# S5 scan of a hybrid encoder: two groups per pass of the array, chunk innermost in the state, one step for both directions

## Chip, cores and metric

The kernel runs on one core of a Trainium2 chip. The metric is the device time of one execution in microseconds. Three runs of the kernel before took 2780.14, 2782.51 and 2787.14 us; the median is 2782.51 us.

## What is computed

The reference is one layer of an encoder over 2304 tokens (256 of a prompt, 2048 of a sample). Its input projection feeds two mixers. One is a gated recurrence (HGRN heads). The other, which the change touches, is a complex diagonal state-space layer (S5) with 32 groups of 16 channels, 64 complex states in each group and two directions. Then come an output projection and an MLP.

```python
bu_re = jnp.einsum('bsgc,gpc->bsgp', u, bb_re)      # and bu_im
_, _, xr, xi = lax.associative_scan(combine, (a_re, a_im, bu_re, bu_im), axis=1)
return jnp.einsum('bsgp,gcp->bsgc', xr, c_re) - jnp.einsum('bsgp,gcp->bsgc', xi, c_im)
...
y_b = _flip(s5_direction(_flip(ug), ...))           # the other direction
```

## The kernel before

Time is cut into 288 chunks of 8 tokens (`NJ`), of which the first 32 (`JP`) are the prompt. The S5 layer then has three parts.

**Chunk inputs** (`s5_in`, lines 552 to 565). For each of 32 groups `g` the sync queue (SP) loads the chunked inputs `ug` (line 559) and, for every second group, the weights `wt` of a pair (line 555). For the real and the imaginary part one matmul (line 562) gives a PSUM tile of 128 partitions by 288 chunks: 64 states of the forward direction over 64 of the backward one. ScalarE copies the upper half into the forward state tile (line 564), VectorE the lower half into the backward one (line 565). A state tile is `[128 partitions, 289 slots, re/im, 16 group pairs]`; a partition is (parity of the group, state). The 288 elements that one copy writes therefore lie 32 words apart, and the 32 elements that belong to one slot lie side by side.

**Scan** (`s5_step`, lines 569 to 580, called in lines 588 to 594). A step takes a direction from one slot to the next with three VectorE operations: `pr = prev * decay`, `cur += pr[0]`, `swp += pr[1]` with real and imaginary parts swapped. The second addition works on the elements that the first has just written, and the next step's product reads them again. While the prompt lasts (k = 1 to 30) an operation carries prompt and sample together: 128 elements in the product, 64 in each addition. For the 224 steps after that (k = 31 to 254) it carries the sample alone: 64 and 32. Both directions step in turn, each in its own tile, so there are six operations per k, and three chained ones always have those of the other direction to be mixed with.

**Outputs** (lines 637 to 657). For every group ScalarE copies the forward states of all slots (line 649) and VectorE the backward ones (line 650) into `xg`, in which the slots lie side by side; three matmuls (lines 652 to 654) add to one PSUM tile, ScalarE copies it out (`yg`, line 656), and the GpSimd queue stores it.

Beside the scan TensorE does the projections of `stage2_v` and `stage2_gq` (lines 599 to 628): 15 tiles of v, then 32 tiles of output gates and queries, whose results ScalarE copies out of three PSUM banks tagged `fl`. The query weights `wqq` (line 625) are split into two parts by ScalarE (`whi`, line 161) and VectorE (`wlo`, line 162). Gate and query tiles of the last two blocks (`late`, line 717) may run once their `h` is loaded, as far as the three `fl` banks go.

The order of the instructions on an engine is not the program's: a planner simulates the program with its own costs (`schedule_with_timeline_sim=True`, line 1340) and puts each instruction where it is ready in that simulation. Each engine then works strictly in that order.

Of the kernel before, what the change touches and what calls it, by code (L numbers as in the profile page):

```python
# [9 lines left out]
F32 = mybir.dt.float32  # L10
# [19 lines left out]
G = 32  # L30
# [14 lines left out]
def hybrid_trunk_kernel(  # L45
# [17 lines left out]
    def order(ins, after, kind=mybir.DependencyClass.NoSync):  # L63
        """Places an instruction behind another one."""
        tc.add_manual_dep(ins.ins, after.ins.name, mybir.DependencyInfo(kind, mybir.DependencyReason.DATA), reason="order of issue")
# [16 lines left out]
    def act(o, i, f, **kw):  # L82
        S.activation(out=o, in_=i, func=f, **kw)  # L83

# [126 lines left out]
    # =====================================================================  # L211
    # stage 1: norm1, h^T, u projection; tables of the S5 layer; chunk inputs
    # =====================================================================
# [62 lines left out]
    def s5_tables():  # L276
# [109 lines left out]
        # decay over one chunk, arranged for the scans: partitions (group parity, state), [kind, re/im, group pair]  # L386
        adec = []
        for d in range(2):
            ad = const.tile([P, 2, 2, G // 2], F32, name=f"adec{d}")
            for q in range(2):  # L390
                o, i = ad[q * 64:(q + 1) * 64], ap[d * 64:(d + 1) * 64, :, LC, q::2]
                for ri in range(2):
                    V.tensor_copy(out=o[:, 0, ri], in_=i[:, 0])
                V.tensor_copy(out=o[:, 1, 0], in_=i[:, 1])
                ts(o[:, 1, 1], i[:, 1], -1.0, op0=ALU.mult)
            adec.append(ad)

        # input matrix of the discretised system
# [16 lines left out]
        # powers arranged by position in the chunk, per direction  # L415
# [14 lines left out]
        # B of the discretised system, and C, with all groups  # L430
# [10 lines left out]
        def quad(o):  # L441
# [9 lines left out]
            # chunk input weights  # L451
# [11 lines left out]
            # output weights  # L463
# [12 lines left out]
            # kernel of every lag: sum over states of B' (C a^n)  # L476
# [29 lines left out]
    # v: blocks from V1 on beside the norms, the others under the scan; NL blocks of queries and output gates  # L506
    # under the S5 outputs; S5 half of the output projection of NE blocks before the backward heads
# [30 lines left out]
    # ---- S5 chunk inputs and states; partitions (group parity, state), [slot, re/im, group pair].  # L538
    # forward: chunk j enters at slot j + 1; backward: at slot j. A chunk's incoming state lies one slot before / after.
# [7 lines left out]
    stt_ = [sp.tile([P, NJ + 1, 2, GH], F32, name=f"st5_{d}") for d in range(2)]  # L547
# [4 lines left out]
    def s5_in(g):  # L552
        if g % 2 == 0:
            wt = tmp2.tile([P, 4, P], F32, name="wt", tag="wt")
            nc.sync.dma_start(out=wt, in_=win_d[g // 2])
            hx["wt"] = wt
        wt = hx["wt"]
        ug = tmp2.tile([P, NJ], F32, name="ug", tag="ug", bufs=4)
        nc.sync.dma_start(out=ug, in_=u_d[g // 8][:, (g % 8) * C16:(g % 8 + 1) * C16, :])
        for ri in range(2):  # L560
            pi = ptile("mm" if (2 * g + ri) % 5 < 3 else "sx", NJ)
            hx["mark", g] = T.matmul(pi, wt[:, 2 * (g % 2) + ri], ug, start=True, stop=True)
            qs = slice((g % 2) * 64, (g % 2 + 1) * 64)
            act(stt_[0][qs, 1:NJ + 1, ri, g // 2], pi[:64], AF.Copy)
            V.tensor_copy(out=stt_[1][qs, 0:NJ, ri, g // 2], in_=pi[64:])

    SL = 2 * GH

    def s5_step(d, src, dst, nq):
        """One chunk of the scan: sample, and beside it prompt (nq = 2) while that lasts."""  # L570
        gap = (JP if d == 0 else NJ - JP) * SL
        s0, d0 = (src * SL, dst * SL)
        prev = view(stt_[d], s0, [[gap, nq], [0, 2], [1, SL]])
        cur = view(stt_[d], d0, [[gap, nq], [1, SL]])
        swp = view(stt_[d], d0, [[gap, nq], [GH, 2], [1, GH]])
        pr = tmp2.tile([P, 2, 2, SL], F32, name="pr", tag=f"pr{d}")[:, :nq]
        ad = view(adec[d], 0, [[0, nq], [SL, 2], [1, SL]])
        tt(pr, prev, ad, ALU.mult)
        tt(cur, cur, pr[:, :, 0], ALU.add)
        tt(swp, swp, view(pr, SL + GH, [[2 * SL, nq], [-GH, 2], [1, GH]]), ALU.add)  # L580

    for g in range(G):
        s5_in(g)
    for j in (0, JP):
        V.memset(stt_[0][:, j], 0.0)
    for j in (JP, NJ):
        V.memset(stt_[1][:, j], 0.0)
    for k in range(1, NJ - JP - 1):
        if k < JP - 1:
            s5_step(0, k, k + 1, 2)  # L590
            s5_step(1, JP - k, JP - k - 1, 2)
        else:
            s5_step(0, JP + k, JP + k + 1, 1)
            s5_step(1, NJ - k, NJ - k - 1, 1)

    # =====================================================================
    # stage 2: v and the output gate of the HGRN heads
    # =====================================================================
# [31 lines left out]
    # =====================================================================  # L630
    # stage 3: S5 outputs
    # =====================================================================
# [4 lines left out]
    for g in range(G):  # L637
# [11 lines left out]
        act(xg[:64], stt_[0][qs, 0:NJ, :, g // 2].rearrange("p j r -> p r j"), AF.Copy)  # L649
        V.tensor_copy(out=xg[64:], in_=stt_[1][qs, 1:NJ + 1, :, g // 2].rearrange("p j r -> p r j"))  # L650
# [70 lines left out]
    for b in range(NB):  # L721
# [33 lines left out]
        # mean square of every token; its root scales this half of the output projection  # L755
# [14 lines left out]
    # =====================================================================  # L770
    # stage 4: HGRN heads, two at a time
    # =====================================================================
# [8 lines left out]
    # lower bounds of the gates: softmax over the layers  # L781
# [20 lines left out]
    def chain(pair, b, h, q, pf, pb):  # L802
        """Gates, and operands of every level: decayed queries and keys."""
# [16 lines left out]
        for m in (1, 2, 4, 8, 16, 32, 64):  # L820
            nb = TB // m
            j = nb // 2
            # rows as the level wants them: by the parity of the block of m tokens
# [26 lines left out]
    def mix(pair, b, h, sel, KQ, ptot):  # L850
        """Attention of the chunks in [source, target] layout, chunk states, forward outputs."""
# [28 lines left out]
        # keys decayed to the chunk's edges -> [token, key], then the states the chunks add  # L880
# [39 lines left out]
    def backward(pair, b):  # L920
        """States from the right, full outputs, norm of every head."""
# [32 lines left out]
    def gate_out(pair, b, outs, r):  # L954
        """Scale by the norm, transpose, gate."""
# [12 lines left out]
    # software pipeline: the projections of the next (block, head) run under the chain of this one  # L968
# [20 lines left out]
    # the output projection of the S5 half and the residual; the heads' half follows  # L989
# [74 lines left out]
    # =====================================================================  # L1064
    # stage 5: output projection of the heads' half, norm2
    # =====================================================================
# [4 lines left out]
    # The products of the MLP by the Winograd form of Strassen's algorithm, one level: seven block products for eight.  # L1071
    # C = A B in blocks: P1 = A11 B11, P2 = A12 B21, P3 = S4 B22, P4 = A22 T4, P5 = S1 T1, P6 = S2 T2, P7 = S3 T3 with
    # S1 = A21 + A22, S2 = S1 - A11, S3 = A11 - A21, S4 = A12 - S2; T1 = B12 - B11, T2 = B22 - T1, T3 = B22 - B12,
    # T4 = B21 - T2; U2 = P1 + P6, U3 = U2 + P7; C11 = P1 + P2, C12 = U2 + P5 + P3, C21 = U3 + P4, C22 = U3 + P5.
    # A is [token, feature], cut by blocks of tokens and halves of the features; B the weights.
# [3 lines left out]
    def s_terms(a, eng=V):  # L1079
        """a: [A21, A11, A12, A22, ...] -> S1 .. S4 behind them."""  # L1080
# [14 lines left out]
    def prep(third, j):  # L1095
        """norm2, transposed: the A operands of the first product, to DRAM."""
# [68 lines left out]
    # =====================================================================  # L1165
    # stage 6: MLP, first product
    # =====================================================================
# [64 lines left out]
    # =====================================================================  # L1232
    # MLP, second product, and the final norm
    # =====================================================================
# [109 lines left out]
```

## Time and profile before

| | |
|---|---|
| median of three runs | 2782.51 us |
| the profiled execution, from first to last instruction | 2785.5 us |
| TensorE matmul busy | 2627.3 us (94%) |
| VectorE busy | 2088.9 us (75%) |
| ScalarE busy | 1411.8 us (51%) |
| chunk inputs, about | 222 to 289 us of the span |
| scan, about | 289 to 516 us |
| S5 outputs, about | 516 to 579 us |

The profiled execution is 3.0 us (0.11%) above the median. Busy times count every instruction from start to end, and neighbours on one engine overlap by a part of their length, so the distance of two starts is shorter than an instruction where nothing is waited for. L12 is line 12 of the kernel, but most VectorE and ScalarE instructions stand under the lines of the helpers `tt` (L68) and `act` (L83); the names of the tiles tell them apart: `pr` and `st` are the scan.

### The profile page before, as it was taken

The page shows a single profiled execution, that of the slowest core. Times are in us where ns is not written, and L with a number is a line of the kernel's source. Part 1 is how long each engine was busy: PE and PEld are TensorE (multiplying, and loading weights), DVE is VectorE, ACT ScalarE, POOL GpSimd, SP SyncE. Part 2 cuts the span into 40 slices and gives each one's busy share as a digit, 9 for nine tenths or more (in the row PEclk, how much of TensorE's full clock was granted, in tenths as well). Part 3 has the DMA queues.
Part 4 walks back from the last instruction along what each step waited for, and adds up shares of the span by engine and source line. Part 5 has one row for each costly group of instructions (what it writes and reads, how often), then busy time and mean ns, then how long its engine had stood idle before and what let it go on. Part 6 is the DMA issues. An engine that isn't in the chain of part 4 may idle for free.

```text
span 2785.5 us, 48587 instructions
## 1 busy us (share of the span) xinstructions
PE 2627.3 (94%) x17590; PEld 2346.9 (84%) x17590; DVE 2088.9 (75%) x5451; ACT 1411.8 (51%) x2632; POOL 665.8 (24%) x853
## 2 busy tenths in 40 slices
PE   6897999889999998999999899989999999999998
PEld 6774899679999887788989899989998888888887
DVE  6666879657899797566999999999986455555564
ACT  5535121476788685345775554564554333344342
POOL 1231233332111112222354344344441000000000
PEclk9999999999999999999999999999999999999999
DMA  9757653687556456799686776687649555765562
GB/s 265 250 189 228 220 179 140 193 252 212 177 182 206 155 192 224 260 327 350 233 281 241 248 276 222 208 283 247 224 149 344 173 170 170 255 229 196 192 218 82
DMA packets 345304, 615.63 MB, mean 221 GB/s; under 512 B 66376, under 2 KB 229576, under 8 KB 345064
## 3 DMA queue, kind: packets, MB, share of 16 engines
q1 hardware_dynamic: 275608, 328.55, 37.6%
q0 software_dynamic: 69456, 283.98, 28.2%
q8 instruction: 139, 2.28, 0.3%
q14 instruction: 101, 0.83, 0.1%
HBM read 409.80 MB, written 202.60 MB: 220 GB/s over the span
## 4 chain that ended last, share of the span: by engine, by line
PE 44%; issue 21%; DVE 19%; ACT 6%; DMA 6%; POOL 4%; SPq 1%; POOLq 0%; ACTq 0%; DVEq 0%
DVE w L68 5%; PE pm L174 5%; PE pm L177 5%; PE pm L178 5%; DVE w1t L68 5%; PE px_g L178 3%; PE px_g L174 3%; PE px_g L177 3%; PE px_fl L174 2%; PE px_fl L178 2%; PE px_fl L177 2%; PE px_tr L174 2%; PE px_tr L178 2%; PE px_tr L177 2%; DVE c L68 2%
## 5 line engine op out<-in xcount | busy, mean ns | idle before, releaser
L68 DVE TENSOR_TENSOR sl<-gt,sh 128x1280 fp32r<-128x1280 f32 (+1 forms) x112 | 153.7, 1373 | 290.7 <-ACT sh L83 289.6
L83 ACT ACTIVATE sh<-gt 128x1280 fp32r<-128x1280 f32 (+1 forms) x112 | 130.7, 1167 | 392.9 <-PE pm L177 150.3
L174 PE MATMUL px_f<-oh,w 128*128 128x384 f32 x672 | 228.0, 340 | 19.8 <-DVE u L68 16.1
L174 PE MATMUL pm<-oh,w 128*128 128x384 f32 x672 | 227.4, 339 | 3.6 <-DVE u L68 2.8
L178 PE MATMUL pm<-oh,w 128*128 128x384 f32 x672 | 227.1, 338 | 2.5 <-DVE w L68 2.4
L177 PE MATMUL px_f<-ol,w 128*128 128x384 f32 x672 | 226.9, 338 | 2.7 <-DVE ol L68 2.7
L177 PE MATMUL pm<-ol,w 128*128 128x384 f32 x672 | 227.6, 339 | 1.7 <-DVE ol L68 1.7
L178 PE MATMUL px_f<-oh,w 128*128 128x384 f32 x672 | 226.5, 337 | 0.9 <-DVE w L68 0.9
L174 PE MATMUL pm<-hh,whi 128*128 128x384 f32 x576 | 200.5, 351 | 9.3 <-ACT sg L83 3.9
L177 PE MATMUL pm<-hl,whi 128*128 128x384 f32 x576 | 200.9, 349 | 0.0
L178 PE MATMUL pm<-hh,wlo 128*128 128x384 f32 x576 | 197.9, 346 | 0.0
L83 ACT ACTIVATE sel<-KQ 128x384 f32<-128x384 f32 (+1 forms) x312 | 168.6, 560 | 52.0 <-DVE KQ L68 50.2
L83 ACT ACTIVATE w<-w1t 128x512 fp32r<-128x512 f32 x192 | 115.4, 620 | 131.7 <-DVE w1t L68 130.0
L83 ACT ACTIVATE c<-c 128x384 f32<-128x384 f32 x192 | 98.2, 516 | 140.2 <-DVE c L68 139.9
L68 DVE TENSOR_TENSOR KQ<-KQ,Fl 128x384 f32<-128x384 f32 x288 | 154.4, 552 | 10.8 <-ACT sel L83 8.7
L1268 POOL DMA_DIRECT2D out_dram<-x x14 | 7.5, 533 | 601.2 <-DVE rs_y L68 484.2
L68 DVE TENSOR_TENSOR w<-w1t,w 128x512 fp32r<-128x512 f32 x192 | 137.2, 716 | 18.4 <-ACT w L83 18.4
L68 DVE TENSOR_TENSOR st<-st,pr 128x32 f32<-128x32 f32 (+1 forms) x1016 | 149.7, 203 | 0.0
L174 PE MATMUL pm<-th,sh 128*128 128x512 f32 x384 | 149.7, 391 | 0.0
L177 PE MATMUL pm<-tl,sh 128*128 128x512 f32 x384 | 149.4, 389 | 0.0
L178 PE MATMUL pm<-th,sl 128*128 128x512 f32 x384 | 149.4, 389 | 0.0
L174 PEld LDWEIGHTS px_f<-oh,w 128*128 128x128 f32 x672 | 126.4, 188 | 24.9 <-issue 19.9
(365 smaller groups left out, 7973.8 us busy)
## 6 DMA issues: line engine op xcount, KB each, us to landing
w1r<-in_w_ff_dram SPq DMA_DIRECT2D x48, 1024.0 KB
gt<-s_d SPq DMA_DIRECT2D x112, 384.0 KB
xg<-in_w_ff_dram SPq DMA_DIRECT2D x80, 512.0 KB
s_d<-his POOLq DMA_DIRECT2D x48, 768.0 KB, 5.0
hh<-h_hi POOLq DMA_DIRECT2D x46, 768.0 KB, 7.5
hl<-h_lo POOLq DMA_DIRECT2D x46, 768.0 KB, 6.7
xg<-t_d SPq DMA_DIRECT2D x64, 512.0 KB
s_d<-hid POOLq DMA_DIRECT2D x48, 576.0 KB, 7.1
```

The costliest lines, as they stand in the source:

```text
L68: ins = V.tensor_tensor(out=o, in0=a, in1=b, op=op)
L83: S.activation(out=o, in_=i, func=f, **kw)
L174: ins = T.matmul(o, ah, bh, start=first, stop=False)
L177: T.matmul(o, ah, bl, start=False, stop=False)
L178: return T.matmul(o, al, bh, start=False, stop=last)
L1268: queue.dma_start(out=rows(yp, ys, t), in_=xt)
```

## The change

The state is one tile `[128, direction, re/im and group pair (32), 289 slots]`, with the slots innermost. `s5_in` takes a pair of groups at once: for each of re/im and direction, two matmuls of 64 weight columns each write the two halves of one PSUM tile, at columns 0 and 64 of the array; the whole tile then goes to the state in one copy, of 128 partitions and 288 elements side by side, by ScalarE for the forward and by VectorE for the backward direction. A step of the scan reads and writes elements that lie 289 words apart. For k = 1 to 30 there is still one step for each direction; for k = 31 to 254 one step of three operations takes both, 128 elements in the product and 64 in each addition. The decay is one tile for both directions. The copies into `xg` read slots that lie side by side. Comments are taken out, so that line numbers stay close.

```diff
-    stt_ = [sp.tile([P, NJ + 1, 2, GH], F32, name=f"st5_{d}") for d in range(2)]
+    SL, NS = 2 * GH, NJ + 1
+    stt_ = sp.tile([P, 2, SL, NS], F32, name="st5")
...
-    def s5_in(g):
...
-        for ri in range(2):
-            pi = ptile("mm" if (2 * g + ri) % 5 < 3 else "sx", NJ)
-            hx["mark", g] = T.matmul(pi, wt[:, 2 * (g % 2) + ri], ug, start=True, stop=True)
-            qs = slice((g % 2) * 64, (g % 2 + 1) * 64)
-            act(stt_[0][qs, 1:NJ + 1, ri, g // 2], pi[:64], AF.Copy)
-            V.tensor_copy(out=stt_[1][qs, 0:NJ, ri, g // 2], in_=pi[64:])
+    def s5_in(g2):
+        wt = tmp2.tile([P, 4, P], F32, name="wt", tag="wt")
+        nc.sync.dma_start(out=wt, in_=win_d[g2])
+        ug = []
+        for g in (2 * g2, 2 * g2 + 1):
+            ug.append(tmp2.tile([P, NJ], F32, name="ug", tag="ug", bufs=4))
+            nc.sync.dma_start(out=ug[-1], in_=u_d[g // 8][:, (g % 8) * C16:(g % 8 + 1) * C16, :])
+        for ri in range(2):
+            for d in range(2):
+                pi = ptile("mm" if (4 * g2 + 2 * ri + d) % 5 < 3 else "sx", NJ)
+                for q in range(2):
+                    hx["mark", 2 * g2 + q] = T.matmul(pi[q * 64:(q + 1) * 64], wt[:, 2 * q + ri, d * 64:(d + 1) * 64], ug[q], start=True, stop=True, tile_position=(0, q * 64))
+                o = stt_[:, d, ri * GH + g2, 1 - d:NJ + 1 - d]
+                if d:
+                    V.tensor_copy(out=o, in_=pi)
+                else:
+                    act(o, pi, AF.Copy)
...
+    def s5_step(src, dst, gap, gap2, ad):
+        prev = view(stt_, src, [[gap, 2], [0, 2], [NS, SL]])
+        cur = view(stt_, dst, [[gap2, 2], [NS, SL]])
+        swp = view(stt_, dst, [[gap2, 2], [GH * NS, 2], [NS, GH]])
+        pr = tmp2.tile([P, 2, 2, SL], F32, name="pr", tag="pr")
         tt(pr, prev, ad, ALU.mult)
         tt(cur, cur, pr[:, :, 0], ALU.add)
-        tt(swp, swp, view(pr, SL + GH, [[2 * SL, nq], [-GH, 2], [1, GH]]), ALU.add)
+        tt(swp, swp, view(pr, SL + GH, [[2 * SL, 2], [-GH, 2], [1, GH]]), ALU.add)
...
         else:
-            s5_step(0, JP + k, JP + k + 1, 1)
-            s5_step(1, NJ - k, NJ - k - 1, 1)
+            f, b = JP + k, DS + NJ - k
+            s5_step(f, f + 1, b - f, b - f - 2, view(adec, 0, [[2 * SL, 2], [SL, 2], [1, SL]]))
...
-        act(xg[:64], stt_[0][qs, 0:NJ, :, g // 2].rearrange("p j r -> p r j"), AF.Copy)
-        V.tensor_copy(out=xg[64:], in_=stt_[1][qs, 1:NJ + 1, :, g // 2].rearrange("p j r -> p r j"))
+        act(xg[:64], stt_[qs, 0, g // 2::GH, 0:NJ], AF.Copy)
+        V.tensor_copy(out=xg[64:], in_=stt_[qs, 1, g // 2::GH, 1:NJ + 1])
```

## Rows read from the trace of the kernel before

**Rows 1.** Busy time of each engine in three stretches: inputs, projections under the scan, outputs.
```profile
core 0: us, PE busy (x) PEld busy (x) DVE busy (x) ACT busy (x) POOL busy (x), PEclk, DMA share, GB/s
222.00:289.00 67.00, 49.50 (x183) 33.24 (x183) 37.67 (x71) 37.77 (x65) 5.39 (x10) 0.97 0.72 226
289.00:499.00 210.00, 206.03 (x1077) 192.18 (x1076) 191.88 (x1384) 37.19 (x67) 60.15 (x95) 0.99 0.50 174
...
517.00:579.00 62.00, 49.51 (x180) 33.80 (x180) 20.54 (x32) 48.20 (x62) 25.12 (x38) 0.96 0.78 234
```
**Rows 2.** Timeline of ScalarE and TensorE, end of scan: start, length, engine, line, tiles [idle before].
```profile
494.50 0.49 ACT L83 ACTIVATE gt<-px_fl 128x384 f32<-128x384 f32 x1 [3.69 <-PE px_fl L178]
498.66 0.49 ACT L83 ACTIVATE gt<-px_fl 128x384 f32<-128x384 f32 x1 [3.67 <-PE px_fl L178]
516.39 1.24 ACT L83 ACTIVATE xg<-st 64x576 f32<-64x576 f32 x1 [17.24 <-DVE st L68]
...
511.88 0.72 PE L652 MATMUL pm<-ug,tm 128*128 128x288 f32 x2
517.68 0.85 PE L653 MATMUL pm<-xg,wc 128*128 128x288 f32 x1 [5.08 <-ACT xg L83]
```
**Rows 3.** Timeline of VectorE, six operations per step: k under 31, then k over 30.
```profile
289.55 0.48 DVE L68 TENSOR_TENSOR pr<-st,adec 128x128 f32<-128x128 f32 x2
289.95 0.62 DVE L68 TENSOR_TENSOR st<-st,pr 128x64 f32<-128x64 f32 x4
290.50 0.48 DVE L68 TENSOR_TENSOR pr<-st,adec 128x128 f32<-128x128 f32 x2
...
359.95 0.36 DVE L68 TENSOR_TENSOR pr<-st,adec 128x64 f32<-128x64 f32 x2
360.22 0.54 DVE L68 TENSOR_TENSOR st<-st,pr 128x32 f32<-128x32 f32 x4
360.68 0.35 DVE L68 TENSOR_TENSOR pr<-st,adec 128x64 f32<-128x64 f32 x2
```
**Rows 4.** Who waited for whom, 289 to 517 us: total, times, longest.
```profile
DVE wlo L68 <- ACT whi L83: 18.1, 2, 9.4
```
**Rows 5.** Groups of 222 to 289 us by shape: count, busy us, mean ns, idle before.
```profile
L83 ACT ACTIVATE st<-pm 64x288 f32<-64x288 f32 x39 | 23.6, 665 | 20.0 <-PE pm L562 19.8
L565 DVE COPY st<-pm 64x288 f32<-64x288 f32 x39 | 23.4, 649 | 17.3 <-ACT st L83 17.0
L562 PE MATMUL pm<-ug,wt 128*128 128x288 f32 x76 | 22.8, 418 | 7.1 <-DMA wt<-win_d 4.6 <-DVE st L565 2.5
```
**Rows 6.** Groups of 516 to 578 us by shape, ScalarE.
```profile
L83 ACT ACTIVATE xg<-st 64x576 f32<-64x576 f32 x32 | 38.5, 1203 | 18.0 <-DVE st L68 17.2
...
L83 ACT ACTIVATE yg<-pm 128x288 f32<-128x288 f32 x29 | 11.6, 399 | 13.0 <-PE pm L654 12.9
```
**Rows 7.** Timeline of the inputs: a load of weights and the matmuls that wait for it.
```profile
248.29 0.32 SPq L555 DMA_DIRECT2D wt<-win_d  x1
...
252.23 1.70 PE L562 MATMUL pm<-ug,wt 128*128 128x288 f32 x6 [1.34 <-DMA wt<-win_d]
```
**Rows 8.** Timeline of TensorE in the heads: matmuls on quarters of the array's columns.
```profile
721.78 1.03 PE L861 MATMUL px_lv<-sel 128*32 128x32 f32 x96
```
**Rows 9.** Timeline of VectorE: a chained pair at the end, and two unrelated neighbours early.
```profile
2778.28 0.15 DVE L198 CAST rs_t<-rs_x 128x1 f32<-128x1 int32 x1
2778.47 0.15 DVE L77 TENSOR_SCALAR rs_y<-rs_t 128x1 int32<-128x1 f32 x1
...
43.12 0.19 DVE L68 TENSOR_TENSOR t<-t,t 128x32 f32<-128x32 f32 x1
43.23 0.18 DVE L288 COPY lim<-px_tr 128x32 f32<-128x32 f32 x1
```
**Rows 10.** The tile `z`: shortest, median and longest ns of an operation, first and last start.
```profile
L68 DVE TENSOR_TENSOR z<-yt,ga x24: 822/862/1585, 589.9 to 676.0; 128x384 f32<-128x384 f32 x24
...
L68 DVE TENSOR_TENSOR z<-z,gate x24: 541/552/560, 611.7 to 704.7; 128x384 f32<-128x384 f32 x24
```
**Rows 11.** Groups of VectorE over the whole span by shape: every second word, in place.
```profile
L68 DVE TENSOR_TENSOR KQ<-KQ,F 128x192 f32<-128x192 f32 x48 | 15.0, 352 | 0.0
```

More of the change, by code (lines that the diff above doesn't have):

```diff
@@ L384, in s5_tables @@
                  b_re, b_im, ap[:, 0, 1:1 + n, :], ap[:, 1, 1:1 + n, :], pw1[:, :n], pw2[:, :n])
-        adec = []
+        adec = const.tile([P, 2, 2, 2, G // 2], F32, name="adec")
         for d in range(2):
-            ad = const.tile([P, 2, 2, G // 2], F32, name=f"adec{d}")
+            ad = adec[:, d]
             for q in range(2):
@@ L395, in s5_tables @@
                 ts(o[:, 1, 1], i[:, 1], -1.0, op0=ALU.mult)
-            adec.append(ad)
         den, nr, cr, ci = pt("den"), pt("nr"), pt("cr"), pt("ci")
@@ L550, in hybrid_trunk_kernel @@
     wg = [col_unit(w_in, 2048 + h * P) for h in range(NH)]
-    def s5_in(g):
[L553 to L559, printed above, removed]
-        for ri in range(2):
-            pi = ptile("mm" if (2 * g + ri) % 5 < 3 else "sx", NJ)
-            hx["mark", g] = T.matmul(pi, wt[:, 2 * (g % 2) + ri], ug, start=True, stop=True)
-            qs = slice((g % 2) * 64, (g % 2 + 1) * 64)
-            act(stt_[0][qs, 1:NJ + 1, ri, g // 2], pi[:64], AF.Copy)
-            V.tensor_copy(out=stt_[1][qs, 0:NJ, ri, g // 2], in_=pi[64:])
@@ L567, in hybrid_trunk_kernel @@
[L567 to L577, printed above, removed]
+    def s5_in(g2):
[5 more added lines that the diff above has]
+            nc.sync.dma_start(out=ug[-1], in_=u_d[g // 8][:, (g % 8) * C16:(g % 8 + 1) * C16, :])
+        for ri in range(2):
+            for d in range(2):
[7 more added lines that the diff above has]
+                    act(o, pi, AF.Copy)
@@ L578, in s5_step @@
+    def s5_step(src, dst, gap, gap2, ad):
[3 more added lines that the diff above has]
+        pr = tmp2.tile([P, 2, 2, SL], F32, name="pr", tag="pr")
         tt(pr, prev, ad, ALU.mult)
         tt(cur, cur, pr[:, :, 0], ALU.add)
-        tt(swp, swp, view(pr, SL + GH, [[2 * SL, nq], [-GH, 2], [1, GH]]), ALU.add)
-    for g in range(G):
-        s5_in(g)
+        tt(swp, swp, view(pr, SL + GH, [[2 * SL, 2], [-GH, 2], [1, GH]]), ALU.add)
@@ L584, in hybrid_trunk_kernel @@
+    for g2 in range(GH):
+        s5_in(g2)
     for j in (0, JP):
-        V.memset(stt_[0][:, j], 0.0)
+        V.memset(stt_[:, 0, :, j], 0.0)
     for j in (JP, NJ):
-        V.memset(stt_[1][:, j], 0.0)
+        V.memset(stt_[:, 1, :, j], 0.0)
+    DS = SL * NS
     for k in range(1, NJ - JP - 1):
         if k < JP - 1:
-            s5_step(0, k, k + 1, 2)
-            s5_step(1, JP - k, JP - k - 1, 2)
-        else:
-            s5_step(0, JP + k, JP + k + 1, 1)
-            s5_step(1, NJ - k, NJ - k - 1, 1)
+            for d in range(2):
+                at, gap = (k, JP) if d == 0 else (DS + JP - k, NJ - JP)
+                s5_step(at, at + 1 - 2 * d, gap, gap, view(adec, d * 2 * SL, [[0, 2], [SL, 2], [1, SL]]))
+        else:
+            f, b = JP + k, DS + NJ - k
+            s5_step(f, f + 1, b - f, b - f - 2, view(adec, 0, [[2 * SL, 2], [SL, 2], [1, SL]]))
```

## Prediction

> **What bounds the kernel now.** I read the busy times by stretch first. From 289 to 499 us, beside the scan, both TensorE (206 of 210 us) and VectorE (192) are full [rows 1]. Which of them sets the end is seen in the timeline at 516 us: TensorE has finished its projections at 511.9, starts the first product that needs no state, and then stands for 5.1 us until `xg` comes; ScalarE's `xg` has waited 17.2 us for the scan's last addition [rows 2]. So the scan ends last, but by little: a shorter scan gains some 6 us before TensorE's own work is the bound, and a longer one costs every microsecond. From 517 to 579 us neither TensorE (49.5 of 62 us) nor ScalarE (48.2) is full; after that TensorE is, so a shift of 579 us goes through to the end.
>
> The scan itself: a step of six operations takes 0.95 us while k is under 31 (from `pr` at 289.55 to `pr` at 290.50) and 0.73 us after (359.95 to 360.68) [rows 3]. 30 and 224 of them make 28.5 + 163 = 191 us of the 228 between 288.6 and 516.4. Of the rest, 18.1 us are two waits of VectorE at `wlo`, for ScalarE's half of the query weights [rows 4].
>
> **Chunk inputs.** Now a copy writes words 32 apart and takes 665 ns on ScalarE and 649 ns on VectorE, 64 each, and VectorE's waits for ScalarE's of the same PSUM tile [rows 5]. After, each engine makes 32 copies into neighbouring words; ScalarE's `yg`, of that shape, takes 399 ns [rows 6]. That takes some 30 us off each engine. But the copies are not all that paces this part. A weight load issued at 248.29 (when its buffer came free) had its matmuls waiting until 252.23 [rows 7]; there are two buffers, so a pair of groups needs about half of these 3.9 us and half of the matmuls' own 2 us, near 3 at best, against 67 / 16 = 4.2 us on the average, in a stretch in which the DMA engines are busy for 0.72 of the time [rows 1]; I take the loads for the larger part of it. The matmuls become twice as many with half the columns. In the heads 96 passes on 32 columns of the array take 1.03 us, 10.7 ns each [rows 8], where a pass over 32 moving columns at the rate of `pm<-ug,wt` (1.70 us for six of 288 [rows 7]) would take 31 ns; so neighbours on other columns do run together, and I take the pair at the price of the one it replaces. I put the part at **-4 us**, between -19 (every pair at 3 us) and +15 (pairs run one after the other: 31 us more on TensorE, half of it in its gaps).
>
> **The scan, k over 30.** Three operations of 128, 64 and 64 elements take the place of six of 64 and 32. This halves the instructions, but each now needs the one right before it. What that costs: in the last norm one-element operations of 0.15 us, each on the result of the one before, start 0.19 us apart, 40 ns more than their length; unrelated 0.19 us neighbours start 0.11 us apart [rows 9]. In the kernel before, an operation of the other direction stands in between and the 0.73 us are the second kind. From 128x384 in 552 ns [rows 10] and 128x192 in 352 ns [rows 11] an addition or product costs 152 ns and 1.04 ns per element: 285 ns for 128 elements, 219 ns for 64. Chained: 325 + 259 + 259 = 0.84 us, already above 0.73.
>
> Then the stride. `z<-yt,ga` reads both sources 48 words apart and takes 822 to 862 ns, `z<-z,gate` of the same shape on neighbouring words 552 [rows 10]: 0.70 to 0.81 ns per element more. The DVE copy that writes 32 words apart fits: 649 ns against 152 + 300 [rows 5]. No row has a read and a write 289 words apart. Below, it costs nothing: `KQ<-KQ,F` in place on every second word takes the 352 ns that the other rows lead to [rows 11]. Above, the penalties of read and write add to 1.5 ns per element. I take 0.75 for the product (reads apart, writes together) and 0.81 for the additions, as `z` is nearest in stride and number of streams: 0.42 + 0.31 + 0.31 = 1.04 us. Over 224 steps that is 234 us instead of 163: **+71 us**, between +26 (no penalty) and +92 (1.14 us).
>
> The Trainium skill's page "Vector Engine (DVE) Microarchitecture Reference", section "Measured stream behaviour on trn2", has a harsher figure for some strides: 2.5 ns per column in place of 1.05 where a stream steps 24 words. By that a step would be an estimated 1.2 us and the scan another 36 us longer; it also lists 1.7 to 2.0 for wider hops, near my rows.
>
> **The scan, k under 31.** Still six operations in two independent chains, so only the stride is added: 0.10 us for each of two products, 0.05 for each of four additions, 0.40 us times 30: **+12 us** (0 to +18).
>
> **VectorE's queue.** `wlo` and the waits on it stay in the queue. The first 9.4 us come because VectorE is there early; a slower VectorE comes later: **-9 us** (-18 to 0). The query projections then get their weights late, but TensorE has over 60 us to spare by then. Query loads on SP and stores on POOL keep their order and only gain time.
>
> **Outputs.** `xg` on ScalarE takes 1203 ns now [rows 6]; on neighbouring words 576 elements should take about 690 (399 plus 288 at 1 ns), 16 us less in all. But TensorE needs six passes of up to 0.28 us [rows 7] per group, as much as ScalarE's two copies take now, and a group takes 62 / 32 = 1.94 us, more than either: **-3 us** (-10 to 0). What was hidden by the scan stays hidden; TensorE now stands idle from about 512 to the scan's end.
>
> **Sum.** -4 + 71 + 12 - 9 - 3 = +67 us on the profiled 2785.5, so 2852.5; less the 3.0 us by which the profile stands over the median, 2849.5 us. The scan would end near 580 us in place of 516.
>
> **Rivals.**
> *Half the operations, half the scan (faster).* If chained operations start as close as unrelated ones and the stride is free, a step costs 0.20 + 2 x 0.14 = 0.48 us, by the starts at 289.55 to 290.50 [rows 3]. The scan is 56 us shorter; the gain stops at the 6 us of TensorE's wait, the 4 of the inputs and some 8 of the outputs' gaps that projections can fill: about 2766 us. It decides if the 40 ns behind the chained pair are not paid. The Trainium skill says so on "VectorE: DVE Perf Modes", section "The DRAIN you can't avoid": with or without semaphores a chain took the same time, and "the semaphore costs nothing extra here". The trace disagrees: 0.19 against 0.11 us [rows 9]. 10%.
>
> *Only one of the two costs is paid (about no change).* Chained but without a stride penalty: +26 - 9 - 4 - 3, 2793 us; with the penalty but not chained (0.30 + 2 x 0.19 = 0.68 us a step): -11 + 12 - 9 - 7, about 2770 us. For it speaks that 352 ns on every second word; against it, `z`. 10%.
>
> *The planned order turns against it (slower still).* Its own simulation orders the instructions. Before, it put the last projections ahead of `xg` on ScalarE, as things then went [rows 2]. If it believes in a scan shorter by the 0.48 us steps (135 us for 191), it puts `xg` into ScalarE's queue at about 445 us. ScalarE then stands there until the scan really ends; three `fl` banks fill, and some ten projections of 4.17 us (494.50 to 498.66 [rows 2]) are left for afterwards: 42 us, of which the outputs' 12.5 us of TensorE gaps [rows 1] take a part. 29 us on top: about 2878 us. 20%.
>
> *The halves do not run side by side.* Then the change doesn't do what its words say: +15 in place of -4, about 2868 us. Against it, 10.7 ns a pass [rows 8]. 5%.
>
> **Numbers.** The forecast has 55%: 2849.5 us. The range takes in the planned order, the bounds of the stride and the upper half of the second rival, not the faster case: 2790 to 2892 us. About 0.3% (8 us) is what a measurement of this kernel can tell from no change. Faster by more: the 10% of the first rival and a little of the second, 0.11. Within: 0.08. Slower: 0.81.
>
> **What would show it.** In the profile after: `pr` and `st` of 128x128 and 128x64 with starts 0.42 and 0.31 us apart and no other operation between; lengths of about 0.38 and 0.27 us; TensorE idle before the first `xg` for tens of microseconds; evictions of 128x288 near 0.4 us; `xg` on ScalarE near 0.7 us. It is wrong if the long steps take 0.7 us or less, if TensorE never waits for the scan, or if ScalarE's last `gt` stand behind `xg`.

## The result, and the profile after

The changed kernel takes **2861.62 us** (median of four runs, 2858.61 to 2869.1) against 2782.17 for the kernel before on the same chip: a ratio of **1.0289**, 95% interval 1.0271 to 1.0308. The change costs 79 us; 2849.5 was predicted, 12 us less. The profiled execution lasts 2861.7 us from first to last instruction, 76.2 more than the one of before.

The busy times by stretch, columns as in [rows 1]: inputs, projections under the scan, the rest of the scan, outputs.

```profile
222.00:289.00 67.00, 55.55 (x271) 31.84 (x270) 13.65 (x32) 12.13 (x30) 3.82 (x8) 0.97 0.63 194
289.00:499.00 210.00, 204.63 (x1049) 188.15 (x1048) 191.83 (x609) 37.28 (x67) 58.44 (x91) 0.98 0.52 178
517.00:585.00 68.00, 4.49 (x26) 4.03 (x24) 61.19 (x199) 0.00 (x0) 0.00 (x0) 0.57 0.02 3
585.00:700.00 115.00, 97.16 (x423) 79.45 (x424) 49.70 (x87) 68.50 (x133) 42.73 (x63) 0.93 0.81 236
```

The third row is new: from 521.5 us until the scan's end VectorE is alone at work, hardly a transfer runs (3 GB/s), and TensorE's granted clock averages 0.57, most of the stretch at the lower of its two levels (1.2 GHz in place of 2.4). The timeline of ScalarE and TensorE at the scan's end shows who waits (answers to [rows 2]):

```profile
508.61 0.49 ACT L83 ACTIVATE gt<-px_fl 128x384 f32<-128x384 f32 x1 [3.67 <-PE px_fl L178]
585.89 2.10 ACT L83 ACTIVATE xg<-st 64x576 f32<-64x576 f32 x3 [76.79 <-DVE st L68]
...
586.63 1.33 PE L656 MATMUL pm<-xg,wc 128*128 128x288 f32 x2 [65.14 <-ACT xg L83]
...
595.05 0.65 PE L655 MATMUL pm<-ug,tm 128*128 128x288 f32 x2
```

The first `xg` comes at 585.9 instead of 516.4, and TensorE stands for 65 us where it stood for 5. The last `gt` lies ahead of `xg`, so nothing that could run under the scan is stuck behind it. VectorE's timeline gives the steps, k under 31 and k over 30 (answers to [rows 3]):

```profile
294.74 0.70 DVE L68 TENSOR_TENSOR pr<-st,adec 128x128 f32<-128x128 f32 x2
295.33 0.83 DVE L68 TENSOR_TENSOR st<-st,pr 128x64 f32<-128x64 f32 x4
296.06 0.70 DVE L68 TENSOR_TENSOR pr<-st,adec 128x128 f32<-128x128 f32 x2
...
439.80 0.40 DVE L68 TENSOR_TENSOR pr<-st,adec 128x128 f32<-128x128 f32 x1
440.23 0.59 DVE L68 TENSOR_TENSOR st<-st,pr 128x64 f32<-128x64 f32 x2
440.86 0.39 DVE L68 TENSOR_TENSOR pr<-st,adec 128x128 f32<-128x128 f32 x1
```

The short step (k under 31) takes 1.32 us (before 0.95), the long one (k over 30) 1.06 us (before 0.73), and in the long one each operation starts only after the one before has ended. Who waited for whom: VectorE from 289 to 590 us (answers to [rows 4]), then TensorE from 222 to 660 us:

```profile
DVE wlo L68 <- ACT whi L83: 0.2, 1, 0.2
...
PE pm L656 <- ACT xg L83: 65.9, 2, 65.1
PE pm L656 <- DMA wc<-wc_d: 10.8, 7, 2.3
```

Groups by shape: evictions and matmuls of the inputs, and ScalarE's copies of the outputs (answers to [rows 5, 6]):

```profile
L83 ACT ACTIVATE st<-pm 128x288 f32<-128x288 f32 x19 | 7.7, 412 | 46.5 <-PE pm L564 37.3 <-PE px_sx L564 4.4 <-DMA win_d<-wt 4.4
L567 DVE COPY st<-pm 128x288 f32<-128x288 f32 x19 | 8.7, 457 | 37.9 <-PE pm L564 37.9
L564 PE MATMUL pm<-ug,wt 128*64 128x288 f32 x145 | 35.0, 412 | 8.2 <-DMA wt<-win_d 4.9 <-DMA ug<-u_d 3.1 <-ACT st L83 0.2
L83 ACT ACTIVATE xg<-st 64x576 f32<-64x576 f32 x32 | 21.8, 683 | 77.5 <-DVE st L68 76.8
```

The copies did get cheap: 0.41 and 0.46 us, half as many, and `xg` 683 ns instead of 1203. But both engines now wait for TensorE in the inputs, and nothing of it reaches the end.

**Where the 76.2 us lie.** The scan begins at 293.43 instead of 288.62 (+4.8). It lasts 292.4 us instead of 227.8 (+64.7): the 30 short steps make +11.6, the waits at `wlo` -17.9, and what is left, +71.0, is the 224 long steps. From the scan's end to the next projection the outputs take 72.3 us instead of 69.1 (+3.2). The last +3.5 come later. All this is read from one profile of each kernel; how far the small parts vary between profiles is said below where they matter.

### The profile page after: what moved, and what is told of

The parts are those of the page before. It is cut to its first block, busy times and chain, and to the rows that moved or that the text cites. A ratio compares the mean times of both kernels' runs of the same rounds, so it can differ in the third digit from the quotient of the medians.

```text
span 2861.7 us, 48080 instructions
## 1 busy us (share of the span) xinstructions
PE 2648.1 (93%) x17718; PEld 2356.1 (82%) x17718; DVE 2119.5 (74%) x4747; ACT 1371.0 (48%) x2600; POOL 664.5 (23%) x853
## 5 line engine op out<-in xcount | busy, mean ns | idle before, releaser
L68 DVE TENSOR_TENSOR st<-st,pr 128x64 f32<-128x64 f32 x568 | 157.8, 296 | 15.3
L1085 POOL TENSOR_TENSOR his<-hid 128x384 f32<-128x384 f32 x96 | 136.6, 1442 | 47.1 <-ACT hid L83 33.1
```

Of the source, the lines that this page charges most:

```text
L68: ins = V.tensor_tensor(out=o, in0=a, in1=b, op=op)
L1085: eng.tensor_tensor(out=a[o], in0=a[x], in1=a[y], op=op)
```

## Experiments

The theory: a long step is longer for two reasons, each paid: three operations that wait for one another, and words 289 apart. The rivals: only the chain, or only the distance. The first three kernels undo one or both in the changed kernel and leave its inputs as they are.

**Words side by side, the chain kept** (`chain_near`).

```diff
-    stt_ = sp.tile([P, 2, SL, NS], F32, name="st5")
+    stt_ = sp.tile([P, 2, NS, SL], F32, name="st5")
...
-        cur = view(stt_, dst, [[gap2, 2], [NS, SL]])
+        cur = view(stt_, dst * SL, [[gap2 * SL, 2], [1, SL]])
```

> The changed kernel with the state turned back so that the 32 elements of a slot lie side by side (copies into the state and out of it step 32 words again); one step of three chained operations for both directions stays. Theory (chain and far words both cost): a step of k over 30 takes 0.84 us in place of 1.04, one of k under 31 0.95 in place of 1.32, the scan is 56 us shorter, the time about 2810 us. Rival 'far words alone' (chaining is free): the step falls to 0.48 us, the scan is over 100 us shorter, TensorE is the bound, about 2775 us. Rival 'chain alone': the step stays at 1.04 us and the time near 2861 us.

**Words far apart, each direction by itself for every k** (`apart_far`): six operations, with a `pr` for each direction.

```diff
+    for k in range(1, NJ - JP - 1):
+        for d in range(2):
...
+                at, gap, nq = (JP + k, JP, 1) if d == 0 else (DS + NJ - k, JP, 1)
+            s5_step(at, at + 1 - 2 * d, gap, nq, view(adec, d * 2 * SL, [[0, nq], [SL, 2], [1, SL]]), d)
```

> The changed kernel with the chunk innermost as it is, but each direction stepping by itself for all k, so that six operations in two independent chains alternate. Theory: no operation waits for its neighbour; a step of k over 30 takes 0.90 us (0.73 and 0.5 to 0.75 ns for each of 256 far elements) in place of 1.04, the time is about 2830 us. Rival 'far words alone': 1.04 us is what the far words cost, and three more operations make it 1.25 us, about 2909 us. Rival 'chain alone': 0.73 us, about 2785 us.

**Both undone** (`apart_near`): the two edits together; the paired inputs stay.

> The changed kernel with both undone: the 32 elements of a slot side by side and each direction by itself, but the inputs still two groups side by side on the array's columns and copied out 128 partitions at a time. Theory: steps of 0.73 and 0.95 us as before the change; what is left of the difference to the kernel before is the inputs, which end some 5 us later: about 2787 us. Rival 'the column halves are the cost': over 2800 us.

One long step in the timeline of VectorE of each: `chain_near`, `apart_far`, `apart_near`.

```profile
440.39 0.29 DVE L68 TENSOR_TENSOR pr<-st,adec 128x128 f32<-128x128 f32 x1
440.71 0.48 DVE L68 TENSOR_TENSOR st<-st,pr 128x64 f32<-128x64 f32 x2
441.23 0.29 DVE L68 TENSOR_TENSOR pr<-st,adec 128x128 f32<-128x128 f32 x1
```

```profile
440.78 0.45 DVE L68 TENSOR_TENSOR pr<-st,adec 128x64 f32<-128x64 f32 x2
441.15 0.60 DVE L68 TENSOR_TENSOR st<-st,pr 128x32 f32<-128x32 f32 x4
441.65 0.44 DVE L68 TENSOR_TENSOR pr<-st,adec 128x64 f32<-128x64 f32 x2
```

```profile
440.81 0.36 DVE L68 TENSOR_TENSOR pr<-st,adec 128x64 f32<-128x64 f32 x2
441.08 0.54 DVE L68 TENSOR_TENSOR st<-st,pr 128x32 f32<-128x32 f32 x4
441.54 0.35 DVE L68 TENSOR_TENSOR pr<-st,adec 128x64 f32<-128x64 f32 x2
```

| kernel | long step, us | VectorE's wait at `wlo`, us | first `xg`, us | median, us | ratio to before (95%) |
|---|---|---|---|---|---|
| changed kernel | 1.06 | 0.2 | 585.89 | 2861.62 | 1.0289 (1.0271 to 1.0308) |
| chain_near | 0.84 | 20.1 | 550.07 | 2827.07 | 1.0167 (1.0144 to 1.019) |
| apart_far | 0.87 | 3.5 | 549.93 | 2813.44 | 1.0128 (1.0102 to 1.0155) |
| apart_near | 0.73 | 20.8 | 524.35 | 2789.98 | 1.0025 (1.0012 to 1.0038) |

Either cost alone makes the kernel slower than both undone, and each is well short of the whole: both rivals fall. With both undone all but 0.25% is gone. The ends of the scan add up. The chain alone puts 0.115 us on a long step, 224 times 26, and the first `xg` comes 25.7 later than in `apart_near`, 1.5 of them because its scan begins later. The distance alone puts 0.14 on the long step (31) and 0.38 on the short one (1.33 against 0.95, 12), gives 17 back at `wlo`, and comes 25.6 later. Both together put 0.33 on the long step, more than the two apart. `hops` below points the same way (the distance costs a chained addition 0.046 us and a free one 0.036); why the two add up to more was not tried.

The medians follow the ends of the scan only roughly: 37 (`chain_near`), 23 (`apart_far`) and 72 us (changed kernel) over `apart_near`, for ends 26, 26 and 62 us later. `chain_near` had been expected at 2810 and `apart_far` at 2830, so their order came out the other way, although the steps came out as expected or 0.03 us shorter. In the profiles the first projection after the outputs still comes 24.5, 23.0 and 62.9 us later; the rest of the difference arises behind it, in the heads and after. The part from the last group of matmuls into the tile `px_ms` (mean squares, the end of the S5 half) to the end differs by up to 11 us between the profiles of these four kernels and by 25 over all the full kernels (2064 to 2089 us), though no edit touches the program there. Executions of one kernel differ too (2775.9 to 2793.9 us for the kernel before), so one profile of each cannot tell a cause there, and it limits what the medians below can settle.

**VectorE's operations by themselves** (`hops`).

> Measures VectorE's operations by themselves; it leaves the whole computation out (the outputs are zeros), so its total time says nothing. Eight sets of 24 in-place additions 128x64 whose words lie 1, 2, 4, 32, 288 or 289 apart, or in neighbours of two or four at 578 and 1156, once each on the result of the one before (the second operand is named chain_...) and once on two tiles in turn (free_...), and two sets of products 128x128 with words 1 or 289 apart. Theory (distance in words and chaining both have a price): near 0.25 us from start to start chained and 0.14 free; 289 apart 0.31 chained and 0.18 free or more; the neighbours of two and four no dearer than near; the product near 0.20, 289 apart 0.30. If the distance costs nothing by itself and it was the other engines' traffic that lengthened the changed kernel's operations: all additions within 0.02 us of near. If chaining costs nothing: chained and free start equally far apart.

The groups by shape of that run, chained additions first, then free ones and products:

```profile
L65 DVE TENSOR_TENSOR xa<-xa,chain_near 128x64 f32<-128x64 f32 x24 | 5.3, 220 | 0.8
L65 DVE TENSOR_TENSOR xa<-xa,chain_two 128x64 f32<-128x64 f32 x24 | 5.4, 226 | 0.8
L65 DVE TENSOR_TENSOR xa<-xa,chain_four 128x64 f32<-128x64 f32 x24 | 6.5, 271 | 0.8
L65 DVE TENSOR_TENSOR xa<-xa,chain_odd 128x64 f32<-128x64 f32 x24 | 6.5, 271 | 0.8
L65 DVE TENSOR_TENSOR xa<-xa,chain_pair 128x64 f32<-128x64 f32 x24 | 5.4, 226 | 0.8
...
L65 DVE TENSOR_TENSOR prod_near<-xa,one 128x128 f32<-128x128 f32 x24 | 4.9, 286 | 0.0
L65 DVE TENSOR_TENSOR prod_odd<-xa,one 128x128 f32<-128x128 f32 x24 | 6.9, 368 | 0.0
```

The distances from start to start tell the price: chained additions at 289 words start 0.306 us apart and the free ones behind them 0.172; with words side by side it is 0.260 and 0.136. So a chain costs 0.12 to 0.13 us for an operation of this size, and the distance 0.04 to 0.05. The distance is paid in full at four words (0.306), and not at all at two (0.260), nor by neighbours of two or four at 578 and 1156 words (0.261, 0.260). The product goes from 0.202 to 0.286. All of that was expected.

In the changed kernel's long steps additions take 281 ns and products 395 (medians) while other engines work, against 271 and 368 here. From 521 us on, where VectorE is alone there too, they take 273 and 380, and the step 1.03 us. `filler`, below, keeps TensorE busy over that time, and the step stays at 1.06. With words side by side no such difference shows: in `chain_near` the step takes 0.85 us before TensorE falls idle and after. So some 0.03 us of the long step were paid for TensorE's work beside it.

**Inputs a group at a time, into the new layout** (`old_inputs`): whole matmuls and four copies of 64 partitions, as before.

```diff
-                    hx["mark", 2 * g2 + q] = T.matmul(pi[q * 64:(q + 1) * 64], wt[:, 2 * q + ri, d * 64:(d + 1) * 64], ug[q], start=True, stop=True, tile_position=(0, q * 64))
+            hx["mark", g] = T.matmul(pi, wt[:, 2 * (g % 2) + ri], ug, start=True, stop=True)
...
+            act(stt_[qs, 0, ri * GH + g // 2, 1:NJ + 1], pi[:64], AF.Copy)
+            V.tensor_copy(out=stt_[qs, 1, ri * GH + g // 2, 0:NJ], in_=pi[64:])
```

> The changed kernel with the input part of before (one matmul on all 128 columns for each group, a copy of 64 partitions by ScalarE and one by VectorE), writing to the new state with the chunk innermost. Theory (column halves run only partly side by side): TensorE's passes for the inputs fall from 63 us busy to about 39, the scan starts some 5 us earlier, the time is about 2855 us. Rival (loads alone pace the inputs): the scan starts within 1 us of where it does and the time stays at 2861 us.

Its scan begins at 287.8 us instead of 293.4 and the first `xg` comes at 579.85, 6.0 sooner. So the halves lose about 6 us in the inputs against whole matmuls, cheaper copies and all. Other profiles bear that out: with halves the scan begins between 291.0 and 295.3 us (five kernels), with whole matmuls and two buffers between 286.7 and 288.6 (three). Against the kernel before (288.6) the cheaper copies by themselves brought 0.8 us. The time is 2859.06 us (1.0284, 1.0264 to 1.0305), not the 2855 expected: 2.6 less, within the intervals, so in the medians the 6 us cannot be seen.

**The column halves by themselves** (`halves`, then `halves_tiles` in the order of the inputs).

> Measures TensorE's column halves by themselves, on zeros; the whole computation is left out (the outputs are zeros), so the total time says nothing. After a lead of whole matmuls (first): 32 matmuls 128x288 on all 128 columns (whole), 32 pairs of halves on columns 0 and 64 in turn (side), 32 whole ones again (again), and 32 pairs with both halves on columns 0 to 63 (same). If two halves run fully side by side: a pair takes as long as one whole matmul (0.49 us for its two passes at full clock). Theory from the changed kernel's inputs (a pair of half passes took 0.34 us against 0.245 for a whole one): side 1.4 times whole, about 0.68 us a pair. If they don't overlap: side as same, 0.98 us a pair. If it was only the waits for loads and evictions that made the inputs' passes look longer: side as whole.

The timeline of TensorE in `halves`: 64 whole passes, 128 half passes side by side, and 128 on the same columns.

```profile
36.76 15.68 PE L73 MATMUL whole<-u,wt 128*128 128x288 f32 x64
52.37 15.74 PE L80 MATMUL side<-u,wt 128*64 128x288 f32 x128
...
83.76 31.25 PE L80 MATMUL same<-u,wt 128*64 128x288 f32 x128
```

Two halves run fully side by side: 15.74 us against 15.68. The factor of 1.4 read off the inputs is no property of the halves.

> Measures the column halves in the order of the changed kernel's inputs (four PSUM tiles for a pair of groups, two matmuls of 64 columns each); all else is left out (the outputs are zeros), so the total time says nothing. Three stretches of 16 pairs after a lead: tiles that nobody reads (alone), tiles copied out by ScalarE and VectorE in turn (evicted), and these with weights and inputs loaded for each pair through the sync queue, two and four buffers (loaded). In the changed kernel the 16 half passes of a pair take about 2.7 us from first to last, where eight whole ones take 1.96. If short PSUM tiles by themselves break the overlap: alone takes 2.7 to 2.9 us a pair (16 pairs: 43 to 47 us). If waits at the borders of tiles and loads break it: alone about 1.96 a pair (16 pairs: 31 us), the loaded stretch's pairs 2.5 us or more from first to last half pass. If it was neither: all three 1.96 to 2.1 from first to last.

Timeline of TensorE: most of the tiles nobody reads, most of those copied out, and pairs with loads (32 half passes are two pairs, 16 are one).

```profile
37.32 30.66 PE L85 MATMUL alone<-u,wt 128*64 128x288 f32 x250
...
68.36 30.66 PE L85 MATMUL evicted<-u,wt 128*64 128x288 f32 x250
...
110.56 5.09 PE L85 MATMUL loaded<-ul,wl 128*64 128x288 f32 x32 [0.91 <-DMA wl<-in_w_in_dram]
...
131.73 5.51 PE L85 MATMUL loaded<-ul,wl 128*64 128x288 f32 x32 [0.63 <-DVE dst L88]
...
144.50 2.67 PE L85 MATMUL loaded<-ul,wl 128*64 128x288 f32 x16 [1.56 <-issue]
```

Without waits 250 half passes take 30.66 us, 0.1215 us from one to the next, copied out or not: neither the short tiles nor the copies break the overlap. Taken pair by pair from the trace, from a pair's first start to its last end, all pairs of these two stretches but the first and the last of each take 2.16 us. With loads, the seven pairs in front of which TensorE stood idle (for a load, for a copy, or for nothing that the profile shows) take 2.67 to 3.15 us, and eight of the nine others 2.34 to 2.59: a pair that begins after a stop overlaps less. In the changed kernel two pairs behind such waits look like this (timeline of TensorE):

```profile
247.14 0.67 PE L564 MATMUL pm<-ug,wt 128*64 128x288 f32 x2 [0.34 <-DMA wt<-win_d]
...
249.47 0.65 PE L564 MATMUL pm<-ug,wt 128*64 128x288 f32 x2
250.38 1.16 PE L564 MATMUL pm<-ug,wt 128*64 128x288 f32 x4 [0.27 <-DMA wt<-win_d]
...
252.40 1.13 PE L564 MATMUL px_sx<-ug,wt 128*64 128x288 f32 x4
```

They take 2.98 and 3.15 us, and the first and the last tile's four passes start 0.24 to 0.26 us apart, one after the other. So a stop costs the overlap at both ends of a pair, as much as a pair of the changed kernel loses. But idle time in front is not all of it. Of the kernel's 16 pairs eight begin behind a wait for `wt`; four that begin without idle time (the first, third, eleventh and thirteenth) take 3.1 to 3.3 us as well, as one of the nine above does (3.16). What takes the overlap there was not tried. In the kernel before the eight whole passes of a pair take 2.2 us, most of them behind a wait too.

**Filler on TensorE while it waits for the scan** (`filler`).

```diff
     hlate = {NB - NL: load_h(NB - NL)}
+    for m in range(384 // 24):
+        pf = ptile("fl", TB)
+        for i in range(24):
+            T.matmul(pf, wqq[3][0][:, i % KD], hlate[NB - NL][0][i // 4 % 2][:, i % 4], start=i == 0, stop=i == 23)
```

> The changed kernel with 384 matmuls of no use (128x384, about 66 us) on TensorE after its last projection, where it stood idle for 65 us; nothing waits for their result. Theory (the outputs' 72.3 us from the scan's end to the next projection, 3 more than before, come from the lower clock after that idle time): the granted clock stays up, the first output passes take 0.65 us for two instead of 1.17, and the outputs take 68 us; the time falls by 4, to about 2857. Rival (the loads pace the outputs whatever the clock): outputs still 72 us, time within 2 us of the changed kernel's.

```profile
584.97 1.33 PE L660 MATMUL pm<-xg,wc 128*128 128x288 f32 x2 [5.66 <-ACT xg L83]
586.09 1.17 PE L661 MATMUL pm<-xg,wc 128*128 128x288 f32 x2
...
592.05 0.65 PE L660 MATMUL pm<-xg,wc 128*128 128x288 f32 x2
592.80 0.55 PE L174 MATMUL px_fl<-hh,whi 128*128 128x384 f32 x1
```

Inconclusive. The clock stayed up under the filler (granted 1.00 from 521 to 579 us), but the filler ended 5.7 us too early, and the first passes again took 1.17 us for two, until 592. It also moved three late projections from ahead of the wait to between the outputs (592.80), so the outputs cannot be compared. The time fell to 2849.62 us (1.0241, 1.0217 to 1.0264), 12 us under the changed kernel; yet its last group of matmuls into `px_ms` starts at 780.6 us, 0.7 later than there. The gain came behind that, for no reason that was shown. The kernel before has the lower level too, after its wait of 5.1 us (timeline of TensorE):

```profile
518.81 1.17 PE L654 MATMUL pm<-xg,wc 128*128 128x288 f32 x2
```

**The layout between the two** (`pairs`): real and imaginary part are neighbours, then the chunk.

```diff
-    stt_ = sp.tile([P, 2, SL, NS], F32, name="st5")
+    stt_ = sp.tile([P, 2, GH, NS, 2], F32, name="st5")
...
+        cur = view(stt_, 2 * dst, [[2 * gap, nq], [2 * NS, GH], [1, 2]])
+        tt(cur, cur, view(pr, SL + 1, [[2 * SL, nq], [2, GH], [-1, 2]]), ALU.add)
```

> A layout between the two: real and imaginary part of a state side by side, then the chunk, then the slot (words of one step: neighbours of two, 578 apart); each direction steps by itself, inputs a group at a time as before, and three buffers for wt and wc3. Evictions and xg then read or write every second word. Theory (neighbours of two cost VectorE no more than words in a row, chained 0.259 against 0.257 us and free 0.136 against 0.136): the long step 0.73 to 0.77 us as before, evictions about 0.41, the first 30 steps some 7 us dearer by their products in two parts, and 2765 to 2778 in all. Rival (the reversed neighbours in the second addition, or the product, cost as much as far words): step 0.82 to 0.87, time 2785 to 2805.

```profile
442.14 0.36 DVE L68 TENSOR_TENSOR pr<-st,adec 128x64 f32<-128x64 f32 x2
442.42 0.54 DVE L68 TENSOR_TENSOR st<-st,pr 128x32 f32<-128x32 f32 x4
442.87 0.22 DVE L68 TENSOR_TENSOR pr<-st,adec 128x64 f32<-128x64 f32 x1
```

The long step takes 0.73 us, the evictions 424 and 461 ns, `xg` 722: cheap copies and the long steps of before at once. It still took 2782.05 us (0.9997, 0.9984 to 1.0009), above the range expected. It also has the third buffers of `deep_loads` below, which by themselves take the kernel before to 0.9959: on top of them this layout loses 0.38%. The short steps, at 1.08 us instead of 0.95, account for 4 of these some 11 us; the rest stayed open. Its scan begins at 280.5 us against 281.2 in `deep_loads`, so the cheap copies brought 0.6 us there: they had not been what bounds that part.

**The kernel before, with its waits taken away one by one**: the low halves of the query weights on GpSimd (`gp_split`), a third buffer for `wt` and `wc3` (`deep_loads`), both (`deep_gp`).

```diff
-    wqq = [col_unit(w_in, h * P, wx if h < 2 else None) for h in range(NH)]
+    wqq = [col_unit(w_in, h * P, wx if h < 2 else None, GP) for h in range(NH)]
...
-            wt = tmp2.tile([P, 4, P], F32, name="wt", tag="wt")
+            wt = tmp2.tile([P, 4, P], F32, name="wt", tag="wt", bufs=3)
...
-            wc = tmp3.tile([P, 2, 2, P], F32, name="wc3", tag="wc3")
+            wc = tmp3.tile([P, 2, 2, P], F32, name="wc3", tag="wc3", bufs=3)
```

> The kernel before, with the low halves of the query weights (4 subtractions) on GpSimd instead of VectorE. Theory (VectorE stands some 18 us in the scan waiting for ScalarE's whi, and the scan's end sets xg, for which TensorE waits 5 us): VectorE's wait is gone, the scan ends up to 18 us sooner, and the time falls by the 5 us for which TensorE waited, to about 2777. Rival (the cover is only moved: outputs then wait for loads): no change within 2 us.

> The kernel before, with three buffers instead of two for the weights of the inputs (wt) and of the outputs (wc3). Theory (TensorE's waits for wt and wc there, 6 and 8 us, are short of a buffer): about 2772 (8 to 14 us less). Rival (the transfers themselves are the limit, or the scan's start only moves against the weights of the queries): within 3 us of before.

> Both of the two edits above on the kernel before. If the waits are independent: the sum of both gains, about 2767. If one hides the other: as the better of the two.

`gp_split` ends the scan at 500.8 us, 15.6 sooner, and takes 2781.48 us (0.9995, 0.9985 to 1.0006): no gain that can be measured, at the most 4 us by the interval. In its profile the gain is there at first: the first output product starts at 511.55 us, 6.1 sooner (only then has TensorE finished its projections), and the last group of matmuls into `px_ms` 9.2 sooner (698.6 against 707.8). Where it is lost behind that was not shown. `deep_loads` takes **2773.69 us** (0.9959, 0.9943 to 0.9975), `deep_gp` 2776.51 (0.9973, 0.996 to 0.9986). The third buffers beat both kernels, the one before by 0.25 to 0.57%, and moving the subtraction adds nothing to it in the medians: `deep_gp` is not the sum (2767). Waits of TensorE in `deep_loads`, 200 to 640 us:

```profile
PE pm L652 <- DMA tm<-k_d: 7.1, 12, 1.3
PE pm L562 <- DMA ug<-u_d: 5.4, 5, 3.6
PE px_sx L562 <- DMA ug<-u_d: 5.2, 5, 3.0
```

The waits for `wt` and `wc` are gone and longer ones for `ug` and `tm` stand in their place. What was gained lies in the inputs: the scan begins 7.4 us sooner (281.2 against 288.6), while from its end to the next projection the outputs take 68.6 us against 69.1.

## Why the prediction came out right

The time lies in the range, on the forecast side, and the scan, nearly all of it, for the reason given. Three smaller terms missed, two of them in sign; +15 and -9 partly cancel, and that the total came within 12 us owes something to this luck. Step by step:

- **The scan, k over 30: +71 predicted, +71 measured.** The step was put at 0.42 + 0.31 + 0.31 us; the starts in the changed kernel lie 0.43, 0.31 and 0.31 apart. Both parts hold by themselves: chained at 0.84 us in a row (predicted 0.84, measured 0.84), and the distance on top. Of its 1.06 us some 0.03 belong to TensorE's work beside it, which the prediction did not have. The rows on `z` [rows 10] were the right ones to go by, and `KQ` on every second word [rows 11] the wrong ones: two words apart cost nothing, four cost all. That `KQ` takes the 352 ns "that the other rows lead to" was circular, as the line had been drawn through it; the 217 ns of 128x64 in the scan before, where the line gives 219, bear it out. The Trainium skill's page "Vector Engine (DVE) Microarchitecture Reference", section "Measured stream behaviour on trn2", gives 2.5 ns per column for a step of 24 words; no run here has that step, but 4, 32, 288 and 289 words all stayed within 0.300 to 0.306 us from one chained addition to the next.
- **The scan, k under 31: +12 predicted, +12 measured**, from 1.33 us a step against 1.35.
- **VectorE's queue: -9 predicted, -18 measured.** I let only the first wait at `wlo` go. The slower VectorE came later to the second one too, and the bound of -18 was reached; this makes the scan's net cost 65 us instead of 74. The scan's end was written as near 580 us; its own terms (516.4 - 4 + 71 + 12 - 9) give 586, and it came at 585.9.
- **Inputs: -4 predicted, +4.8 measured.** The failed step is "I take the pair at the price of the one it replaces". I had checked it on passes that follow each other without a wait [rows 8], and there it holds (15.74 against 15.68 us). In the inputs a pair without a wait inside takes 2.7 to 3.3 us where an unbroken stream needs 2.2. Stops make for much of that, as `halves_tiles` shows; the whole of it was not explained. That not the copies pace the part was right: by themselves they bring 0.6 to 0.8 us (`pairs` against `deep_loads`, `old_inputs` against before), a third buffer for the loads 7.4. So 30 us less of copying on each engine brought next to nothing.
- **Outputs: -3 predicted, +3.2 measured.** The copy came out as worked out (683 ns for 690), but it was again not the bound. That cheaper copies bring nothing here is shown: with `xg` at 683 ns the outputs take 72.3, 69.8 and 68.4 us (changed kernel, `old_inputs`, `apart_far`), with `xg` at 1.2 us 69.1, 69.7 and 71.0 (before, `chain_near`, `apart_near`). The +3.2 lies within that spread. TensorE's lower clock level after the wait (1.17 us for two passes, until 594) is no full cause either: `old_inputs` has the same outputs after a wait of 68 us and takes 69.8, and the kernel before has the lower level too after its 5 us, until 522. What makes single profiles differ by some 4 us there stayed open.
- **Total: +67 predicted, +76 in the profiles, +79 in the medians.** Inputs and outputs were each wrong in sign, +15 together, the queue gave 9 back, and 3.5 us came after the outputs, unexplained. The further 3 between profiles and medians lie within the spread of executions.

The rivals: *half the operations, half the scan* fell with the chained starts (its 2766 us should have read 2764.5 by its own terms). The Trainium skill's "VectorE: DVE Perf Modes", section "The DRAIN you can't avoid", would have an operation on the one before cost nothing extra by its semaphore; measured, it starts 0.260 us after it and an unrelated one 0.136. *Only one of two costs* fell with `chain_near` and `apart_far`. *The planned order* did not come about: the last `gt` at 508.6 lies ahead of `xg`. *Halves not side by side* is half true: they are in an unbroken stream, and only in part in the inputs.

## What to carry to other kernels

Fewer, larger operations can lose on VectorE if each needs the one just before it: here two independent chains in turn hid 0.12 us behind every operation, and merging them laid it bare. In a serial scan the layout belongs to the scan; neighbours of two kept its long steps at the old price and made the copies cheap as well, but no time was won by it. Before making copies cheaper, look at what their engine waits for afterwards: here it was loads in the inputs, and a third buffer brought more (0.41%) than every rearrangement tried.

## What the runs showed of the hardware that was not expected

- Two halves of TensorE's columns run side by side at no cost in an unbroken stream (0.123 us per half pass, 0.245 per whole one), but a pair of groups begun after a stop takes 2.67 to 3.15 us instead of 2.16. How the overlap is lost there was not tried.
- On VectorE the price of distance is a step: nothing at two words, all of it at four (0.260 and 0.306 us from one chained 128x64 addition to the next), and the same at 289.
- Operations on far words took longer while TensorE worked (a long step 1.06 us against 1.03 in the changed kernel once TensorE stood idle, 1.06 with `filler`), those on words side by side did not (0.85 and 0.85 in `chain_near`).
- TensorE's granted clock was at its lower level, 1.17 us for two passes, after waits of 5.1 us (before) and 5.7 us (`filler`) as after one of 65 us.
